# Two output projections of a hybrid decoder by one level of Strassen's algorithm, with weight sums made in DRAM

## The chip, the core and the metric

The kernel runs on one core of a Trainium2 chip. The metric is device microseconds (us) of one execution; lower is better. The core has TensorE (PE, with its weight loads PEld), VectorE (DVE), ScalarE (ACT), GpSimd (POOL) and SyncE (SP, which issues the DMAs of the kernel before). "Granted clock" is TensorE's clock as the records show it, as a share of 2.4 GHz.

## The reference

Two decoder layers over 1024 tokens of width 1024, in float32. Layer 0 is a gated DeltaNet, layer 1 a Mamba-2 SSD mixer. Each ends in an output projection of 2048 channels to 1024, which is what is changed here, then a residual sum and the next norm.

```python
def reference(x, norm_w, ...):                       # x: 1 x 1024 x 1024
    hid = rmsnorm(x, norm_w[0])
    o = gated_deltanet_core(hid, gdn_w_in, ...)      # 1024 x 2048, 16 heads of 128
    x = x + o @ gdn_w_out                            # gdn_w_out: 2048 x 1024
    hid = rmsnorm(x, norm_w[1])
    y = ssd_core(hid, ssd_w_in, ...)                 # 1024 x 2048, 8 groups of 256
    x = x + y @ ssd_w_out                            # ssd_w_out: 2048 x 1024
    return rmsnorm(x, final_norm_w)
```

## The kernel before

Every large matmul is made of three: an operand is split into a rounded part (hi, float32r, a cast on ACT) and the rest (lo, a subtraction on DVE; `split`, lines 86 and 87), and hi x hi, hi x lo and lo x hi are summed in PSUM. Tokens come in 8 chunks n of 128.

The stages are: norm of x into `hid` (hi and lo, transposed, in the pool `apool`, tags a0 to a3); the DeltaNet stage in the pool `gw` (8 head pairs g; for each a scan over the 8 chunks, with the inverse and the input projections of later pairs set between its steps, "SIJ"); the first output projection; the SSD stage in the pool `sw` (8 groups g, each a scan over the chunks); the second output projection. In the scan of the last pair or group there are no input projections left; only the z matmuls (lines 227 to 229) of its 8 chunks stand between the steps of chunks 0 to 3. A scan ends for each chunk in `store`: transposes, a copy into `yg`, and a DMA to y0d (line 691) or y1d (line 923). In the DeltaNet scan the recurrence runs over lines 626 (S times k), 629, 634, 637, 643 and 649 (new S); its output over 661 to 680.

`out_proj` (line 321) takes each half of 512 outputs in turn (nh), in it the 8 chunks n, in them 4 blocks kq of 512 channels: it loads a block of y (line 340) and splits it, and makes 12 matmuls of 128 x 512 (lines 347 to 349). The weights of the first half lie in apool and those of the second in `bpool`, which is opened when gw is closed and stays open through the SSD stage. With nh = 0 the sums go to DRAM (`keep`: x1d or xfd); with nh = 1 a row of 1024 is complete, is normed (`rms_first`, `rms_second`) and goes to `on_rows`: transposes into `hid2` through `to_hid` in the middle, the output at the end. Rows, norms and the norm weights nw lie in `nrm1` and `nrm2`.

Pools lie on a stack: one that is opened after another has been closed takes the same bytes. Instructions are ordered on each engine by a planner that simulates the program; an engine then runs its own list strictly in order. Tiles of one tag share a fixed number of buffers (`bufs`).

## Time and profile before

| | |
|---|---|
| Median of 3 runs | 1993.75 us (1992.37 to 1995.21) |
| The profiled execution | 1990.66 us, span of the core 1989.0 us |
| Mean granted clock | 0.987 |
| Busy share of the span | PE 96%, PEld 82%, DVE 66%, ACT 53%, POOL 21% |
| DMA | 34.2% of 16 engines, all of it on one queue (SP's) |

The span runs from the first to the last instruction of the core in one profiled execution. A matmul's end is modelled and matmuls are pipelined, so that their listed durations overlap. An idle engine costs nothing unless another waits for it.

### The profile page before, as it was taken

What the parts mean: (1) busy time and instruction counts of PE and PEld (TensorE: products, weight loads), DVE (VectorE), ACT (ScalarE), POOL (GpSimd) and SP (SyncE); (2) the same over time, 40 slices, a digit from 0 to 9 for tenths busy, and PEclk for the clock granted to TensorE, in tenths of its full rate; (3) what the DMA queues carried; (4) which work ended last, traced back from release to release, by engine and by line L of the source; (5) the groups of instructions that cost most, each with busy time, mean ns of one, the idle gap of its engine ahead of it and who ended that gap; (6) DMA issues with size and microseconds to landing.
All of it is one profiled execution on the core that took longest, in us unless ns stands there. A gap on an engine that the chain in (4) does not pass through costs nothing.

```text
span 1989.0 us, 36043 instructions
## 1 busy us (share of the span) xinstructions
PE 1919.1 (96%) x12974; PEld 1639.7 (82%) x12974; DVE 1305.7 (66%) x2915; ACT 1063.4 (53%) x2893; POOL 411.6 (21%) x818
## 2 busy tenths in 40 slices
PE   7997999999999999999999999999999999999998
PEld 5786888888888888897778788888888888888886
DVE  6797685778677776844354676657666676767333
ACT  5635656575656666564343554544555555555332
POOL 1101211212122212100000032423333243332000
PEclk9997999999999999999999999999999999999999
DMA  4421323232232323235574232222222223236654
GB/s 141 117 54 49 98 56 84 67 78 75 57 93 52 99 49 105 58 94 157 152 221 133 64 91 80 69 84 80 64 80 57 80 75 83 78 104 195 203 170 142
DMA packets 284789, 193.35 MB, mean 97 GB/s; under 512 B 65425, under 2 KB 246338, under 8 KB 284610
## 3 DMA queue, kind: packets, MB, share of 16 engines
q1 hardware_dynamic: 284610, 191.05, 34.2%
q8 instruction: 102, 1.67, 0.4%
q14 instruction: 77, 0.63, 0.1%
HBM read 159.34 MB, written 31.65 MB: 96 GB/s over the span
## 4 chain that ended last, share of the span: by engine, by line
PE 75%; DMA 9%; DVE 7%; ACT 4%; POOL 2%; issue 2%; SPq 1%; POOLq 0%; DVEq 0%; ACTq 0%
PE ps_proj L165 9%; PE ps_proj L166 9%; PE ps_proj L167 9%; PE ps_proj L347 6%; PE ps_proj L349 6%; PE ps_proj L348 5%; PE ps_proj L227 5%; PE ps_proj L228 4%; PE ps_proj L229 4%; DMA gcrow<-gcr_s 2%; PE ps_tr L66 2%; PE ps_pt L66 2%; DMA X<-xd 2%; DVE acc L204 2%; PE ps_sc L895 1%
## 5 line engine op out<-in xcount | busy, mean ns | idle before, releaser
L165 PE MATMUL ps_proj<-hid_h,wh 128*128 128x512 f32 x1024 | 412.9, 403 | 3.4 <-ACT acc L200 3.2
L167 PE MATMUL ps_proj<-hid_h,wl 128*128 128x512 f32 x1024 | 404.9, 395 | 0.0
L166 PE MATMUL ps_proj<-hid_l,wh 128*128 128x512 f32 x1024 | 403.6, 394 | 0.0
L227 PE MATMUL ps_proj<-zh,hid_h 128*128 128x256 f32 x1024 | 300.5, 293 | 1.0 <-DVE z L234 1.0
L229 PE MATMUL ps_proj<-zh,hid_l 128*128 128x256 f32 x1024 | 295.4, 288 | 0.0
L228 PE MATMUL ps_proj<-zl,hid_h 128*128 128x256 f32 x1024 | 295.4, 288 | 0.0
L165 PEld LDWEIGHTS ps_proj<-hid_h,wh 128*128 128x128 f32 x1024 | 192.7, 188 | 43.9 <-ACT acc L200 4.0
L167 PEld LDWEIGHTS ps_proj<-hid_h,wl 128*128 128x128 f32 x1024 | 192.5, 188 | 40.3
L166 PEld LDWEIGHTS ps_proj<-hid_l,wh 128*128 128x128 f32 x1024 | 192.9, 188 | 35.4
L347 PE MATMUL ps_proj<-woh,yh 128*128 128x512 f32 x512 | 205.2, 402 | 4.6 <-ACT yh L86 3.2
L348 PE MATMUL ps_proj<-wol,yh 128*128 128x512 f32 x512 | 204.4, 400 | 0.8 <-DVE wol L87 0.7
L349 PE MATMUL ps_proj<-woh,yl 128*128 128x512 f32 x512 | 203.1, 399 | 0.8 <-DVE yl L87 0.7
L227 PEld LDWEIGHTS ps_proj<-zh,hid_h 128*128 128x128 f32 x1024 | 196.3, 192 | 6.0 <-DVE z L234 2.3
L228 PEld LDWEIGHTS ps_proj<-zl,hid_h 128*128 128x128 f32 x1024 | 196.4, 192 | 3.0
L229 PEld LDWEIGHTS ps_proj<-zh,hid_l 128*128 128x128 f32 x1024 | 196.4, 192 | 0.3
L204 DVE SCALAR_TENSOR_TENSOR acc<-raw,cw_ssd,acc 128x512 f32<-128x512 f32 x192 | 156.5, 815 | 45.2 <-ACT acc L202 42.5
L86 ACT CAST yh<-yr 128x512 fp32r<-128x512 f32 x128 | 79.1, 619 | 142.2 <-PE ps_proj L348 90.8
L87 DVE TENSOR_TENSOR yl<-yr,yh 128x512 fp32r<-128x512 f32 x128 | 89.0, 696 | 98.7 <-ACT yh L86 98.3
L204 DVE SCALAR_TENSOR_TENSOR acc<-raw,cw_gdn,acc 128x512 f32<-128x512 f32 x192 | 145.9, 761 | 11.8 <-ACT acc L200 10.2
L87 DVE TENSOR_TENSOR wl<-wr,wh 128x512 fp32r<-128x512 f32 x128 | 89.3, 698 | 68.3 <-ACT wh L86 67.7
L317 POOL TENSOR_SCALAR_AFFINE_SELECT gcrow<-gcrow 128x512 f32<-128x512 f32 x128 | 92.1, 722 | 197.1 <-DMA gcrow<-gcr_g 141.8
L676 POOL TENSOR_SCALAR so<-so,cq 128x2 f32<-128x2 f32 x64 | 27.3, 426 | 462.7 <-ACT yn L675 462.7
(240 smaller groups left out, 3872.0 us busy)
## 6 DMA issues: line engine op xcount, KB each, us to landing
wr<-in_gdn_w_in_dram SPq DMA_DIRECT2D x96, 256.0 KB, 3.0
wr<-in_ssd_w_in_dram SPq DMA_DIRECT2D x96, 256.0 KB, 2.9
gcrow<-gcr_g SPq DMA_DIRECT2D x64, 256.0 KB, 3.6
yr<-y0d SPq DMA_DIRECT2D x64, 256.0 KB, 3.4
gcrow<-gcr_s SPq DMA_DIRECT2D x64, 256.0 KB, 3.9
yr<-y1d SPq DMA_DIRECT2D x64, 256.0 KB, 3.2
y0d<-yg SPq DMA_DIRECT2D x64, 128.0 KB, 1.9
wr<-in_gdn_w_out_dram SPq DMA_DIRECT2D x32, 256.0 KB, 3.5
```

The source lines that it names most:

```text
L87: nc.vector.tensor_tensor(out=lo, in0=src, in1=hi.bitcast(F32), op=ALU.subtract)
L165: nc.tensor.matmul(pt[0:nco], hi[:, j, 0:nco], xh[:, j, :], start=first, stop=False)
L166: nc.tensor.matmul(pt[0:nco], hi[:, j, 0:nco], xl[:, j, :], start=False, stop=False)
L167: nc.tensor.matmul(pt[0:nco], lo[:, j, 0:nco], xh[:, j, :], start=False, stop=last)
L204: nc.vector.scalar_tensor_tensor(out=acc, in0=raw[:, k:k + 512], scalar=cw[:, k * 32 + ti:k * 32 + ti + 1], in1=acc, op0=ALU.mult, op1=ALU ...
L227: nc.tensor.matmul(pt, xh, zh[:, k, :], start=k == 0, stop=False)
L228: nc.tensor.matmul(pt, xh, zl[:, k, :], start=False, stop=False)
L229: nc.tensor.matmul(pt, xl, zh[:, k, :], start=False, stop=k == KT - 1)
L317: nc.gpsimd.affine_select(out=t, in_=t, pattern=[[0, 4], [1, P]], compare_op=ALU.is_ge, fill=-1e30, base=0, channel_multiplier=-1)
L347: nc.tensor.matmul(pt, yh[:, j, :], hi[:, j, :], start=first, stop=False)
L348: nc.tensor.matmul(pt, yh[:, j, :], lo[:, j, :], start=False, stop=False)
L349: nc.tensor.matmul(pt, yl[:, j, :], hi[:, j, :], start=False, stop=last)
```

## The change

Tokens, channels and outputs are each cut in two. Instead of 8 products of halves there are 7, each of 512 tokens x 1024 channels x 512 outputs (8 pieces j of 128 channels, 4 banks p of 128 tokens), of sums of quarters of y and sums of quarters of the weights. The sums of y are made on the way: in a tile T and on POOL and DVE (`y_form`). Four sums of weight quarters for each projection (s1 to s4) are made in DRAM while the DeltaNet stage runs: `weight_sums` yields 11 DMAs from POOL's queue for each projection, 4 that copy 2 MB and 7 that add 2 MB to what is there; one is traced at every second slot of the scans. Weights are split again for each product instead of once.

The products alternate between two sets of four PSUM banks (U and V). Sums of products are kept in rows of 1024 that start from the residual (8 tiles of 512 KB, loaded when product 0 is done), and in u. Products 5 and 6 complete four rows each. All tiles of the new `out_proj` but the raw loads are in nrm1 and nrm2; bpool is opened for the SSD stage alone, and closed with it. y is stored in four quarters of 1024 channels x 512 tokens, so that its rows are 2 KB instead of 512 bytes.

The diff, without lines that are only removed from `out_proj`:

```diff
--- before.py
+++ after.py
...
-    def rms_first(pool, xrow):
-        xn = pool.tile([P, D], F32, tag="xn", name="xn")
-        ss = st.tile([P, 2], F32, tag="ss2", name="ss2")
-        nc.scalar.activation(xn[:, 0:512], xrow[:, 0:512], AF.Square, accum_out=ss[:, 0:1])
+    def rms_first(sq, xrow, c):
+        ss = st.tile([P, 2], F32, tag="ss2", name="ss2", bufs=NT)
+        nc.scalar.activation(sq, xrow[:, c * 512:(c + 1) * 512], AF.Square, accum_out=ss[:, 0:1])
         nc.gpsimd.tensor_scalar(out=ss[:, 0:1], in0=ss[:, 0:1], scalar1=1.0 / D, scalar2=EPS, op0=ALU.mult,
                                 op1=ALU.add)
-        return xn, ss
-
-    def rms_second(xrow, xn, ss, nw, emit):
-        nc.scalar.activation(xn[:, 512:1024], xrow[:, 512:1024], AF.Square, accum_out=ss[:, 1:2])
+        return ss
+
+    def rms_second(xrow, xn, ss, nw, emit, c):
+        cs = slice(c * 512, c * 512 + 512)
+        nc.scalar.activation(xn[:, cs], xrow[:, cs], AF.Square, accum_out=ss[:, 1:2])
...
     def to_hid(kh, xn, hid, n):
-        pt = (ps_pt, ps_sc)[kh]()
+        pt = (ps_tr, ps_sc)[kh]()
...
-    def out_proj(yd, w_out, resid, wpools, npool, nw, on_rows, keep):
...
+    def weight_sums(w_out, nm):
+        X = lambda c, k: w_out[k * 1024:(k + 1) * 1024, c * 512:(c + 1) * 512]
+        parts = {"s1": ((1, 0), (1, 1)), "s2": ((1, 0), (1, 1), (0, 0)), "s3": ((0, 0), (1, 0)),
+                 "s4": ((0, 1), (1, 0), (1, 1), (0, 0))}
+        forms = {f"x{c}{k}": X(c, k) for c in range(2) for k in range(2)}
+        for f in parts:
+            forms[f] = tc.dram_tile([1024, 512], F32, name=f"wo_{nm}{f}")
+        def steps():
+            for i in range(4):
+                for f, p in parts.items():
+                    if i < len(p):
+                        if i == 0:
+                            nc.gpsimd.dma_start(forms[f], X(*p[0]))
+                        else:
+                            nc.gpsimd.dma_start(forms[f], X(*p[i]), accum_op=ALU.add)
+                        yield
+        return forms, steps()
+    def out_proj(yd, forms, resid, npool, nw, on_rows):
+        rows = {t: [npool.tile([P, D], F32, tag="xr", name="xrow", bufs=NT) for _ in range(4)] for t in range(2)}
+        tok = lambda t, p: p + 4 * (1 - t)
+        Tt = npool.tile([P, 8, 512], F32, tag="T", name="Tt", bufs=1)
+        sums = {}
+        def load_y(k, t, j):
+            yr = cv.tile([P, 512], F32, tag="acc", name="yr", bufs=3)
+            nc.sync.dma_start(yr, yd[k, 1 - t][j * P:(j + 1) * P, :])
+            return yr
+        def y_form(i, j):
+            if i == 0:
+                return load_y(0, 0, j)
+            if i == 3:
+                return load_y(1, 0, j)
+            if i == 5:
+                return load_y(1, 1, j)
+            if i == 4:
+                a, b = load_y(1, 1, j), load_y(0, 1, j)
+                nc.gpsimd.tensor_tensor(out=a, in0=a, in1=b, op=ALU.subtract)
+                return a
+            d = Tt[:, j, :]
+            if i == 1:
+                a, b = load_y(0, 0, j), load_y(0, 1, j)
+                nc.gpsimd.tensor_tensor(out=d, in0=a, in1=b, op=ALU.subtract)
+            elif i == 2:
+                a = load_y(1, 1, j)
+                nc.vector.scalar_tensor_tensor(out=d, in0=d, scalar=-1.0, in1=a, op0=ALU.mult, op1=ALU.subtract)
+            else:
+                a = load_y(1, 0, j)
+                nc.vector.scalar_tensor_tensor(out=d, in0=d, scalar=-1.0, in1=a, op0=ALU.mult, op1=ALU.subtract)
+            return d
+        def pieces(i, j):
+            raw = wring.tile([P, 512], F32, tag="wr", name="wr", bufs=3)
+            nc.sync.dma_start(raw, forms[wf[i]][j * P:(j + 1) * P, :])
+            wh = npool.tile([P, 512], F32R, tag="woh", name="woh", bufs=4)
+            wl = npool.tile([P, 512], F32R, tag="wol", name="wol", bufs=4)
+            split(wh, wl, raw)
+            y = y_form(i, j)
+            yh = npool.tile([P, 512], F32R, tag="yh", name="yh", bufs=4)
+            yl = npool.tile([P, 512], F32R, tag="yl", name="yl", bufs=4)
+            split(yh, yl, y)
+            return wh, wl, yh, yl
+        def mac(pt, pc, p, first, last):
+            wh, wl, yh, yl = pc
+            c = slice(p * P, (p + 1) * P)
+            nc.tensor.matmul(pt, yh[:, c], wh, start=first, stop=False)
+            nc.tensor.matmul(pt, yh[:, c], wl, start=False, stop=False)
+            nc.tensor.matmul(pt, yl[:, c], wh, start=False, stop=last)
+        def product(i, banks, done):
             for j in range(4):
+                pc = pieces(i, j)
+                for p in range(4):
+                    mac(banks[p], pc, p, j == 0, False)
+            pcs = [pieces(i, j) for j in range(4, 8)] if i == 6 else None
+            if i == 6:
+                for p in range(4):
                     for j in range(4):
+                        mac(banks[p], pcs[j], p, False, j == 3)
+                    done(p, banks[p])
+                return
+            for j in range(4, 8):
+                pc = pieces(i, j)
+                for p in range(4):
+                    mac(banks[p], pc, p, False, j == 7)
+            for p in range(4):
+                done(p, banks[p])
+        def put(t, p, c, pt, op):
+            v = rows[t][p][:, c * 512:(c + 1) * 512]
+            if op == ALU.add:
+                nc.vector.tensor_tensor(out=v, in0=pt, in1=v, op=ALU.add)
+            else:
+                nc.vector.tensor_tensor(out=v, in0=v, in1=pt, op=ALU.subtract)
+        def finish(t, p, c):
+            xrow = rows[t][p]
+            on_rows(tok(t, p), xrow, lambda emit: rms_second(xrow, npool.tile([P, D], F32, tag="xn", name="xn"),
+                                                             sums[t, p], nw, emit, c))
+        def first(t, p, c):
+            sums[t, p] = rms_first(npool.tile([P, 512], F32, tag="sq", name="sq", bufs=1), rows[t][p], c)
+        wf = ("x00", "s1", "s2", "x01", "s3", "s4", "x11")
+        U = lambda: [ps_proj(), ps_proj(), ps_pt(), ps_pt()]
+        V = lambda: [ps_tr(), ps_tr(), ps_sc(), ps_sc()]
+        u = npool.tile([P, 4, 512], F32, tag="u", name="u", bufs=1)
+        def put_u(t, p, c, op):
+            v = rows[t][p][:, c * 512:(c + 1) * 512]
+            nc.gpsimd.tensor_tensor(out=v, in0=v, in1=u[:, p, :], op=op)
+        def grow(p, pt):
+            nc.vector.tensor_tensor(out=u[:, p, :], in0=pt, in1=u[:, p, :], op=ALU.add)
+        def d0(p, pt):
+            for t in range(2):
+                nc.sync.dma_start(rows[t][p], resid(tok(t, p)))
+            nc.scalar.copy(u[:, p, :], pt)
+            put(0, p, 0, pt, ALU.add)
+        def d1(p, pt):
+            put(1, p, 0, pt, ALU.add)
+            put(1, p, 1, pt, ALU.subtract)
+        def d2(p, pt):
+            grow(p, pt)
+            put_u(1, p, 0, ALU.add)
+        def d3(p, pt):
+            put(0, p, 0, pt, ALU.add)
+            first(0, p, 0)
+        def d4(p, pt):
+            grow(p, pt)
+            put_u(1, p, 1, ALU.subtract)
+            first(1, p, 1)
+            put_u(0, p, 1, ALU.subtract)
+        def d5(p, pt):
+            put(1, p, 0, pt, ALU.add)
+            finish(1, p, 0)
+        def d6(p, pt):
+            put(0, p, 1, pt, ALU.subtract)
+            finish(0, p, 1)
+        for i, done in enumerate((d0, d1, d2, d3, d4, d5, d6)):
+            product(i, V() if i % 2 else U(), done)
...
-    yd0 = [tc.dram_tile([2048, P], F32, name=f"y0d{n}") for n in range(NT)]
+    def y_dram(nm):
+        return {(k, t): tc.dram_tile([1024, 512], F32, name=f"{nm}{k}{t}") for k in range(2) for t in range(2)}
+
+    def y_cut(yd, g, n):
+        return yd[g // 4, n // 4][(g % 4) * 256:(g % 4 + 1) * 256, (n % 4) * P:(n % 4 + 1) * P]
+
+    yd0, yd1 = y_dram("y0d"), y_dram("y1d")
+    wo0, steps0 = weight_sums(gw_out, "g")
+    wo1, steps1 = weight_sums(sw_out, "s")
...
-                nc.sync.dma_start(yd0[n][g * 256:(g + 1) * 256, :].rearrange("(h p) t -> p h t", p=P), yg)
+                nc.sync.dma_start(y_cut(yd0, g, n).rearrange("(h p) t -> p h t", p=P), yg)
...
             for slot in range(8):
+                if slot % 2:
+                    next(steps0 if g < 3 else steps1, None)
                 for c in "SIJ":
...
-    bpool = ctx.enter_context(tc.tile_pool(name="bpool", bufs=2))
     hid2 = hid_tiles(apool)
 
     with tc.tile_pool(name="nrm1", bufs=2) as nrm:
         nw = load_nw(nrm, norm_w[1])
 
         def rows_mid(n, xrow, norm):
-            nc.sync.dma_start(x1d[n][:, 512:1024], xrow[:, 512:1024])
+            nc.sync.dma_start(x1d[n], xrow)
             norm(lambda kh, xn: to_hid(kh, xn, hid2, n))
 
-        out_proj(yd0, gw_out, lambda n: x[n * P:(n + 1) * P, :], (apool, bpool), nrm, nw, rows_mid, x1d)
-
-    yd1 = [tc.dram_tile([2048, P], F32, name=f"y1d{n}") for n in range(NT)]
-    xfd = [tc.dram_tile([P, D], F32, name=f"xfd{n}") for n in range(NT)]
-
-    with tc.tile_pool(name="sw", bufs=2) as sw:
+        out_proj(yd0, wo0, lambda n: x[n * P:(n + 1) * P, :], nrm, nw, rows_mid)
+
+    with tc.tile_pool(name="bpool", bufs=2) as bpool, tc.tile_pool(name="sw", bufs=2) as sw:
...
-        out_proj(yd1, sw_out, lambda n: x1d[n], (apool, bpool), nrm, nw, rows_last, xfd)
+        out_proj(yd1, wo1, lambda n: x1d[n], nrm, nw, rows_last)
```

## Rows read from the trace of the kernel before

**Rows 1.** the page, part 1: engine, busy us (share of the span) x instructions.
```profile
PE 1919.1 (96%) x12974; PEld 1639.7 (82%) x12974; DVE 1305.7 (66%) x2915; ACT 1063.4 (53%) x2893; POOL 411.6 (21%) x818
```

**Rows 2.** windows: stretch, length, busy us of PE, PEld, DVE, ACT, POOL; clock, DMA, GB/s.
```profile
160.00:200.00 40.00, 31.28 (x162) 25.81 (x163) 34.47 (x105) 23.05 (x87) 5.95 (x13) 0.78 0.10 32
...
985.00:1030.00 45.00, 42.15 (x171) 31.62 (x171) 23.86 (x38) 21.39 (x41) 2.02 (x6) 0.96 0.86 248
...
1844.00:1960.00 116.00, 116.00 (x504) 94.42 (x503) 45.54 (x69) 36.97 (x72) 5.40 (x17) 1.00 0.62 184
```

**Rows 3.** instructions of lines L349 and L229 (the latter from 840 to 900 us).
```profile
L349 PE MATMUL ps_proj<-woh,yl x512: 387/395/629, 886.0 to 1981.5; 128*128 128x512 f32 x171
...
L229 PE MATMUL ps_proj<-zh,hid_l x66: 273/282/387, 839.7 to 885.5; 128*128 128x256 f32 x66
```

**Rows 4.** windows of line L347 alone: busy us (x instructions) of PE and PEld, clock, DMA.
```profile
889.00:985.20 96.20, 44.11 (x107) 20.52 (x107) 0.98 0.49 148
...
1797.00:1843.30 46.30, 21.45 (x55) 10.16 (x54) 1.00 0.71 213
```

**Rows 5.** timeline of PE, 163 to 190 us: start us, us, what, idle before.
```profile
173.50 1.22 PE L634 MATMUL ps_sc<-vpp,nte 128*128 128x128 f32 x4 [0.80 <-DVE vpp L629]
...
179.29 0.71 PE L634 MATMUL ps_sc<-vpp,nte 128*128 128x128 f32 x4 [0.70 <-DVE vpp L629]
```

**Rows 6.** chain that ended last, 880 to 1120 us: start us, us, what.
```profile
891.78 0.44 PE ps_sc L634 x4
...
933.49 0.45 PE ps_sc L634 x4
...
1107.77 0.44 PE ps_sc L66 x4
```

**Rows 7.** timeline of all engines, 963 to 968 us.
```profile
963.76 0.42 DVE L671 TENSOR_TENSOR o<-ps_sc,o 128x256 f32<-128x256 f32 x1 [0.67 <-ACT o L670]
...
965.65 0.61 PE L634 MATMUL ps_sc<-vpp,nte 128*128 128x128 f32 x4
...
966.48 0.62 DVE L680 SCALAR_TENSOR_TENSOR yn<-o,so,z 128x128 f32<-128x128 f32 x2 [2.29 <-POOL so L678]
```

**Rows 8.** chain that ended last, 955 to 1000 us.
```profile
981.22 3.95 DMA y0d<-yg
...
985.27 0.63 ACT woh L86
```

**Rows 9.** instructions on tile nw: count, ns min/median/max, first to last start.
```profile
L91 SPq DMA_DIRECT2D nw<-in_norm_w_dram x2: 345/382/420, 1.2 to 985.2; - x2
...
L91 SPq DMA_DIRECT2D nw<-in_final_norm_w_dram x1: 333/333/333, 1844.0 to 1844.0; - x1
```

**Rows 10.** groups by line: xcount, busy us, mean ns of one, idle before.
```profile
L87 DVE TENSOR_TENSOR yl<-yr,yh 128x512 fp32r<-128x512 f32 x128 | 89.0, 696 | 98.7 <-ACT yh L86 98.3
...
L887 POOL TENSOR_TENSOR S<-S,egl_s 128x256 f32<-128x256 f32 x48 | 37.8, 788 | 24.0 <-DVE S L888 17.1 <-DVE S L885 2.8 <-PE ps_tr L66 2.5
```

**Rows 11.** timeline of all engines, 1790 to 1846 us.
```profile
1793.92 0.27 PE L895 MATMUL ps_sc<-xs,mt 128*64 128x64 f32 x1
...
1827.77 0.27 PE L895 MATMUL ps_sc<-xs,mt 128*64 128x64 f32 x1
...
1832.84 0.35 DVE L910 TENSOR_SCALAR yn<-y,so 128x256 f32<-128x256 f32 x1
```

**Rows 12.** DMA issues: count, KB each, median us to landing.
```profile
yr<-y1d SPq DMA_DIRECT2D x64, 256.0 KB, 3.2
...
xrow<-in_x_dram SPq DMA_DIRECT2D x8, 512.0 KB, 7.9
```

**Rows 13.** timeline of POOL, first 8 us.
```profile
1.49 0.10 POOL L194 MEMSET raw<- 128x3 f32 x1
...
6.07 0.19 POOL L99 TENSOR_SCALAR rr<-ss 128x1 f32<-128x1 f32 x1 [4.25 <-ACT xn L97]
```

More of the change, by code (lines that the diff above doesn't have):

```diff
@@ L319, in gc_rows @@
         return t
-    def out_proj(yd, w_out, resid, wpools, npool, nw, on_rows, keep):
-        def load_kq(nh, kq):
-            hi = wpools[nh].tile([P, 4, 512], F32R, tag=("a0", "a0", "a1", "a1")[kq], name="woh", bufs=2)
-            lo = wpools[nh].tile([P, 4, 512], F32R, tag=("a2", "a2", "a3", "a3")[kq], name="wol", bufs=2)
-            for j in range(4):
-                k = kq * 4 + j
-                raw = wring.tile([P, 512], F32, tag="wr", name="wr", bufs=3)
-                nc.sync.dma_start(raw, w_out[k * P:(k + 1) * P, nh * 512:(nh + 1) * 512])
-                split(hi[:, j, :], lo[:, j, :], raw)
-            return hi, lo
-        w = {(0, kq): load_kq(0, kq) for kq in range(4)}
-        for nh in range(2):
-            for n in range(NT):
-                if nh == 0 and n >= 4:
-                    w[1, n - 4] = load_kq(1, n - 4)
-                pt = ps_proj()
-                for kq in range(4):
-                    yr = cv.tile([P, 4, P], F32, tag="acc", name="yr", bufs=3)
-                    nc.sync.dma_start(yr, yd[n][kq * 512:(kq + 1) * 512, :].rearrange("(k p) t -> p k t", p=P))
-                    yh = wring.tile([P, 4, P], F32R, tag="wh", name="yh")
-                    yl = wring.tile([P, 4, P], F32R, tag="wl", name="yl")
-                    split(yh, yl, yr)
-                    hi, lo = w[nh, kq]
-                    for j in range(4):
-                        first, last = kq == 0 and j == 0, kq == 3 and j == 3
-                        nc.tensor.matmul(pt, yh[:, j, :], hi[:, j, :], start=first, stop=False)
-                        nc.tensor.matmul(pt, yh[:, j, :], lo[:, j, :], start=False, stop=False)
-                        nc.tensor.matmul(pt, yl[:, j, :], hi[:, j, :], start=False, stop=last)
-                xin = cv.tile([P, 512], F32, tag="th", name="xin")
-                nc.sync.dma_start(xin, resid(n)[:, nh * 512:(nh + 1) * 512])
-                if nh == 0:
-                    nc.vector.tensor_tensor(out=xin, in0=pt, in1=xin, op=ALU.add)
-                    nc.sync.dma_start(keep[n][:, 0:512], xin)
-                else:
-                    xrow = npool.tile([P, D], F32, tag="xr", name="xrow")
-                    nc.sync.dma_start(xrow[:, 0:512], keep[n][:, 0:512])
-                    xn, ss = rms_first(npool, xrow)
-                    nc.vector.tensor_tensor(out=xrow[:, 512:1024], in0=pt, in1=xin, op=ALU.add)
-                    on_rows(n, xrow, lambda emit: rms_second(xrow, xn, ss, nw, emit))
@@ L922, in store @@
                                          scale=snw[:, 2 * g + i:2 * g + i + 1])
-                nc.sync.dma_start(yd1[n][g * 256:(g + 1) * 256, :].rearrange("(h p) t -> p h t", p=P), yg)
+                nc.sync.dma_start(y_cut(yd1, g, n).rearrange("(h p) t -> p h t", p=P), yg)
             S = None
```

## Prediction

> **What bounds the kernel now.** I read the page's busy table first: PE is busy 1919 of 1989 us, POOL a fifth of that [rows 1]. PE's figure overstates its work, since matmuls overlap, so the second view is the windows: in a stretch that holds nothing but the second output projection, 504 matmuls took 116.0 us, 0.230 us each [rows 2], although one of them is listed with 0.395 [rows 3]. At that pace PE has no free time there. Each of the projections' three lines has 512 matmuls [rows 3], so a projection has 768, 177 us of pure matmul time.
>
> Third, where that work lies. L349 starts first at 886.0 us, just behind the last matmul for z (L229, 885.5), and last at 1981.5 [rows 3]. So the first projection starts while head pair 7 of the DeltaNet scan is still going, and the second while group 7 of the SSD scan is. L347 alone has 107 matmuls between 889 and 985.2, and 55 between 1797 and 1843.3 [rows 4]; with its two partners that is 321 and 165, 74 and 38 us of PE work, laid between the steps of a scan that by itself leaves PE waiting. What such a scan looks like with hardly any filler stands at 160 to 200 us: PE busy 31 of 40 us, DVE 34, the mean granted clock 0.78, so part of it at 1.2 instead of 2.4 GHz [rows 2]; there two steps of the recurrence (L634) start 5.8 us apart [rows 5]. With the projection between them, two of the last steps took 32 us (933.49 to 965.65) [rows 6, 7].
>
> Fourth, why the projection can start there. Its first-half weights lie in apool, over the hid tiles. The second-half weights lie in bpool, on the bytes of the closed pool gw, and the chain shows their first cast at 985.27, directly behind the last store of the scan, 981.22 + 3.95 us [rows 8]. The loads of nw for nrm1 and nrm2, which lie on bytes of the same kind, issue at 985.2 and 1844.0, each as its scan's last store lands [rows 9]. So here every tile of a new pool waited for the last user of the pool whose bytes it took.
>
> **The change part by part.** *Matmuls.* Seven products of 8 x 4 x 3 are 672 for 768: 96 fewer per projection, 22.1 us, 44.2 for both. Same shapes and the same order of weight loads, so the same 0.230.
>
> *The cover that goes.* woh, wol, yh and yl now come from nrm1 and nrm2, and T, u, the rows and xn too. By [rows 8, 9] nothing of product 0 can be split before the scan's last store has landed. The first two products need only channels of groups 0 to 3, which were written long before, but that frees nothing. In the first projection chain step 2 stands at 891.78 [rows 6]; I put it at 890 without matmuls ahead of it. Five unfilled steps of 5.9 end at 919.5. From step 7 to the store: L634 to its output about 2.5 us, the output tile to yn 3.3 (963.76 to the end of the L680 pair, 966.48 + 0.62) [rows 7], transposes and the copy about 0.7, the store 3.95 [rows 8], semaphores: 11 us. Before, from 965.65, it was 19.5 us with filler; that is the upper bound. So the pool opens at 930.5, and after two casts of 0.63 [rows 8] PE starts at 932. Then 2 us for a clock that has fallen, 672 x 0.230 = 155, and 7 us of transposes (16 groups of 0.44): 1096. Before, the last transposes end at 1108.2 [rows 6], since the second-half weights also cost a stall there (985 to 1030: 171 matmuls and transposes in 45 us, DMA share 0.86 [rows 2]). Gain of the first: 12 us, not 22.
>
> In the second, main step 3 is at 1793.92 and step 7 at 1827.77 [rows 11], filled steps 8.5 us apart. POOL has three products of 0.79 in a step, 2.4 us, as the floor [rows 10]. I take 4.85, a little under the middle, as most of a filled step is filler: step 7 at 1813.3. Step 7 to the last yn was 5.4 us before (1827.77 to 1832.84 + 0.35) [rows 11], transposes and copies 1.2, the store 4: 1823.9. PE starts at 1825.4, and 1.5 us of slow clock and 155 us end at 1982, where the old one ended. Gain: none. Together 12 us.
>
> *Feeding the products.* A product lasts 22.1 us, a piece (12 matmuls) 2.76. A piece takes two casts of 0.63 on ACT and two subtractions of 0.70 on DVE [rows 8, 10], well inside. Products 2 and 3 add eight combinations on T at the same 0.70: DVE 16.8 us, and the puts of the product before up to 5.6 more. Product 6 of the first projection is worse: after product 5 four rows are finished at once, 4 x (0.7 + 1.4 + 1.4) = 14 us of DVE ahead of its own 11.2, more than 22.1. Products 1 and 4 need two y loads in three buffers, each held for a landing of 3.2 us [rows 12], a POOL subtraction (about 1.5 us, twice the 0.79 of half the size [rows 10]) and a split: about 4 us a piece where PE wants 2.76, of which the four pieces of lead hide only part. Product 0 starts while eight rows of 512 KB are fetched too; such eight took 7.9 us each at the start [rows 12]. Below, all of it hides in the lead but 3 us for both projections. Above: product 1 late by 11, 4 by 4, 6 by 4 and the start by 4, 23 in the first and 12 in the second. I take 10 and 6, nearer the middle, since the start empties the lead.
>
> *Weight sums.* 22 transfers of 2 MB leave from POOL's queue, 14 of them accumulating. No row shows a DMA from POOL. Its list is not in program order: the memset of the first convolution (L194) stands at 1.49, before the norm's L99 at 6.07, and a transfer without a predecessor may be placed as early as that [rows 13]. Below, they cost nothing: POOL is idle 79% [rows 1]. Above: 2 MB at 248 GB/s [rows 2] is 8.5 us, and if POOL or a scan's small loads are held for that long, a quarter of 22 times reaches PE: 47 us. I take 6, near the lower end, as only the stretches with a wait for POOL or a load feel it.
>
> The Trainium skill, "SBUF — State Buffer", section "SBUF: two separate sides", has a rule against this change: a DMA issued from GpSimd has its descriptors written by GpSimd, and a VectorE instruction that holds the shared port keeps it from writing them. No run here shows it. The page's example (620 ns alone, 3100 beside a copy) would give, as an estimate from that page, 22 x 2.5 = 55 us on POOL's queue, and a time up to 2053 if all of that came through.
>
> *The rest.* The stores and reloads of keep and xfd that go cost PE nothing now. bpool opens after nrm1; its first user gtmp waited for the end of the same matmuls before. What follows the last matmul keeps its parts.
>
> **Sum.** -12 + 16 + 6 = +10 us. The profiled execution took 1990.66, of which 1989.0 is span; the runs' median is 1993.75, 0.15% higher, and the same work stands in both, so I add to the median: 2004.
>
> **Rivals.** *The lead hides the feeding* (faster). Stalls of 3 us for both, weight sums free: -9; if the scan's tail is 3 us shorter in each than I make it: -15, so 1979 to 1985. For: PE had no gap in 1844 to 1960 with 184 GB/s moving [rows 2]. Against: products 1 and 4 want half as much again. It decides from the point where feeding and weight sums together cost under 8 us. *The scan keeps its cover* (faster still): if a tile waited only for its own bytes, product 0 would fill some 21 us of each scan: 10 - 42, 1962. [rows 8, 9] speak against it. *POOL's queue becomes a bound* (much slower): an accumulating transfer must wait for the one before it on the same sum, and that wait stands ahead of gcrow masks, conv edges and norms in POOL's queue, for which ACT and DVE wait: 47 instead of 6, 2045. For: POOL's list may take them early; against: other sums lie between two steps of one. *All cancels*: within 0.2%.
>
> **How the numbers follow.** 0.2% (4 us) is about what a measurement of this kernel can tell from no change. Forecast (lost cover, some feeding stalls) 0.46, POOL's queue 0.14: slower 0.60. Cancelled 0.15. Hidden feeding 0.20 and kept cover 0.05: faster 0.25. The forecast's own range is 1998 to 2025. To leave out no more than 2 in 10, the range reaches into the hidden feeding and up to the upper price of the weight sums: 1978 to 2045.
>
> **What will show it.** Right: the first cast of woh directly behind the last y store; PE nearly idle for 30 us ahead of it, with a fallen clock; about 165 us from the first to the last matmul of a projection; gaps in products 1, 4 and 6. Wrong: product matmuls before the last store; projections of 156 us with no gap; a DeltaNet stage stretched by more than 10 us.

## The result and the profile after

The changed kernel took 2173.24 us (median of four runs, 2168.95 to 2182.44), the kernel before 1993.06 us beside it: a ratio of 1.0909, interval [1.0871, 1.0947], or 180 us more. The forecast was 2004, its range ended at 2045. The profiled execution took 2182.44 us with a span of 2180.7, where before had 1989.0: 191.7 more.

The page of the changed kernel, its busy table, the slices that matter and its DMA queues:

```profile
PE 1914.4 (88%) x12782; PEld 1621.3 (74%) x12782; DVE 1385.1 (64%) x3011; ACT 1083.8 (50%) x2933; POOL 524.0 (24%) x896
...
PE   2722789999999999999779999999999999997897
...
PEclk6766789999999999999999999999999999997999
DMA  9999531323232222222366623232222213215665
...
q1 hardware_dynamic: 237762, 201.54, 31.8%
q0 software_dynamic: 18784, 46.14, 9.8%
```

PE has 192 instructions fewer than in [rows 1], as forecast, and is busy 88% instead of 96%. The loss stands in the first four slices (218 us): PE at 2 to 7 tenths, the DMA engines at 9. Two later dips, in slices 20 and 21 and in 37 and 38, are the starts of the two projections. q0 is the queue of POOL's transfers: 9.8% of 2180.7 us is 214 us of all sixteen DMA engines.

The windows of the start, first of the changed kernel, then of the kernel before (columns as in [rows 2]: length; busy us and count of PE, PEld, DVE, ACT, POOL; clock, DMA share, GB/s):

```profile
0.00:20.00 20.00, 3.31 (x16) 3.07 (x16) 4.55 (x5) 7.81 (x13) 10.53 (x26) 0.94 0.92 345
40.00:60.00 20.00, 2.47 (x6) 1.25 (x7) 0.69 (x4) 0.40 (x1) 2.58 (x2) 0.50 1.03 321
120.00:140.00 20.00, 0.00 (x0) 0.00 (x0) 0.00 (x0) 0.00 (x0) 1.39 (x1) 0.50 1.12 228
180.00:200.00 20.00, 0.00 (x0) 0.00 (x0) 0.75 (x1) 0.00 (x0) 1.51 (x3) 0.54 1.13 207
```

```profile
0.00:20.00 20.00, 7.82 (x32) 6.28 (x32) 9.98 (x13) 11.05 (x20) 4.89 (x21) 1.00 0.76 259
40.00:60.00 20.00, 20.00 (x102) 16.35 (x102) 14.70 (x45) 10.32 (x18) 0.23 (x2) 1.00 0.20 54
120.00:140.00 20.00, 19.51 (x101) 16.50 (x100) 18.50 (x43) 8.26 (x16) 0.57 (x4) 1.00 0.27 54
```

From 120 to 140 us no compute engine does anything but POOL, which issues one transfer, and the granted clock stands at 0.50, the 1.2 GHz level, behind stretches in which PE had little to do. The same 20 us of before are nearly full. The transfers themselves, grouped by line and tile (durations in ns are POOL's time to issue one; below them the landing times, minimum, median and maximum, first of the copies, then of the accumulating ones):

```profile
L335 POOL DMA_DIRECT2D wo_gs<-in_gdn_w_out_dram x4: 777/784/1042, 1.8 to 4.3; - x4
L335 POOL DMA_DIRECT2D wo_ss<-in_ssd_w_out_dram x4: 774/774/774, 5.1 to 7.3; - x4
...
DMA to landing us min/median/max: 16.1/42.8/69.4
```

```profile
L337 POOL DMA_DIRECT2D wo_gs<-in_gdn_w_out_dram x7: 1272/1337/1413, 18.2 to 196.3; - x7
...
DMA to landing us min/median/max: 25.2/76.9/93.4
```

All eight copies have left by 8 us, as early as [rows 13] allowed. The last accumulating one leaves at 216.5. What the loads of SP find meanwhile, from the DMA issues of 0 to 220 us (count, size, median us to landing), before and after:

```profile
wr<-in_gdn_w_in_dram SPq DMA_DIRECT2D x25, 256.0 KB, 2.9
```

```profile
q0 software_dynamic: 17762, 44.08, 91.5%
q1 hardware_dynamic: 9698, 9.07, 14.6%
...
wr<-in_gdn_w_in_dram SPq DMA_DIRECT2D x11, 256.0 KB, 19.0
gcrow<-gcr_g SPq DMA_DIRECT2D x4, 256.0 KB, 21.1
```

A weight load of 256 KB lands in 19.0 us instead of 2.9, and 11 of them are issued in the time of 25. The last y0d store is issued at 1072.3 us (981.2 before, with the projection's filler among the steps), the first projection's last matmul ends at 1261.2 (before 1099.5, +161.7), the second's at 2169.1 (1981.9, +187.2), the span at 2180.7 (+191.7). By the matmuls of L165, which both kernels have, 152 us are lost by 269 us; most of the rest goes in the second projection. So the DeltaNet stage was stretched by far more than the 10 us that the prediction named as a sign of being wrong.

### The profile page after: what moved, and what is told of

The parts are those of the page before. It is cut to its first block, busy times and chain, and to the rows that moved or that the text cites. A ratio compares the mean times of both kernels' runs of the same rounds, so it can differ in the third digit from the quotient of the medians.

```text
span 2180.7 us, 36007 instructions
## 1 busy us (share of the span) xinstructions
PE 1914.4 (88%) x12782; PEld 1621.3 (74%) x12782; DVE 1385.1 (64%) x3011; ACT 1083.8 (50%) x2933; POOL 524.0 (24%) x896
## 5 line engine op out<-in xcount | busy, mean ns | idle before, releaser
L165 PE MATMUL ps_proj<-hid_h,wh 128*128 128x512 f32 x1024 | 415.5, 406 | 50.9 <-ACT wh L86 45.9
L229 PE MATMUL ps_proj<-zh,hid_l 128*128 128x256 f32 x1024 | 297.8, 291 | 0.0
L165 PEld LDWEIGHTS ps_proj<-hid_h,wh 128*128 128x128 f32 x1024 | 194.8, 190 | 93.3 <-ACT wh L86 47.0
L229 PEld LDWEIGHTS ps_proj<-zh,hid_l 128*128 128x128 f32 x1024 | 197.6, 193 | 0.5
L184 ACT ACTIVATE th<-acc 128x512 f32<-128x512 f32 x128 | 80.1, 627 | 119.8 <-DVE acc L204 119.4
L197 ACT COPY raw<-ps_proj 128x512 f32<-128x512 f32 x128 | 74.3, 580 | 99.6 <-PE ps_proj L167 95.1
L86 ACT CAST wh<-wr 128x512 fp32r<-128x512 f32 x128 | 78.3, 615 | 88.9 <-PE ps_proj L166 56.5
L609 DVE TENSOR_TENSOR tm<-Dt,X 128x2 f32<-128x2 f32 (+30 forms) x248 | 86.9, 350 | 45.3 <-POOL X L598 40.0
L87 DVE TENSOR_TENSOR wol<-wr,woh 128x512 fp32r<-128x512 f32 x112 | 86.3, 774 | 44.7 <-ACT woh L86 44.4
```

The costliest lines, as they stand in the source:

```text
L86: nc.scalar.copy(hi, src)
L87: nc.vector.tensor_tensor(out=lo, in0=src, in1=hi.bitcast(F32), op=ALU.subtract)
L165: nc.tensor.matmul(pt[0:nco], hi[:, j, 0:nco], xh[:, j, :], start=first, stop=False)
L184: nc.scalar.activation(th, src, AF.Tanh, scale=0.5)
L229: nc.tensor.matmul(pt, xl, zh[:, k, :], start=False, stop=k == KT - 1)
L609: nc.vector.tensor_tensor(out=tv, in0=Dt[:, r0:, s:], in1=X[:, s:s + 1, s:].to_broadcast([P, nr, nj]), op=ALU.mult)
```

## The experiments

Every kernel is compared with the kernel before on its own chip (1992.5 to 1999.8 us there). "Over before" is the difference of the medians; the ratio is estimated from all the runs of both kernels and need not be exactly that of the medians. Besides the changed kernel itself, only e1, e11 and e14 use the whole sums; e2 makes them, and nothing reads them. The others leave some or all of the sums out, so that some of their products are of other weights; they are there for their times.

| run | us | over before | ratio, interval |
|---|---|---|---|
| changed kernel | 2173.24 | +180.2 | 1.0909 [1.0871, 1.0947] |
| e2, sums alone in the kernel before | 2143.12 | +143.3 | one run |
| e3, no sums | 2034.40 | +34.6 | 1.0179 [1.0162, 1.0196] |
| e4, copies, nothing accumulates | 2152.86 | +153.1 | one run |
| e5, eight copies | 2061.66 | +66.2 | one run |
| e10, eight big copies | 2144.10 | +145.2 | one run |
| e1, sums spread over the DeltaNet stage | 2092.24 | +92.4 | 1.0464 [1.0443, 1.0485] |
| e11, small sums over both scans, nine y buffers | 2042.76 | +43.9 | 1.0211 [1.0190, 1.0233] |
| e6, no sums, nine y buffers | 2001.08 | +5.7 | 1.0035 [1.0024, 1.0047] |
| e7, no sums, product 0 as cover | 2032.75 | +37.3 | 1.0189 [1.0170, 1.0208] |
| e9, e6 and e7 | 2010.80 | +11.9 | 1.0052 [1.0031, 1.0072] |
| e8, e6, rows by program order | 2003.46 | +8.0 | 1.0043 [1.0029, 1.0058] |
| e12, e6, rows behind y loads | 2000.04 | +7.5 | 1.0043 [1.0028, 1.0057] |
| e13, e6, rows behind weight loads | 2016.93 | +17.9 | 1.0085 [1.0070, 1.0100] |
| e14, e11 and e13 | 2043.91 | +44.9 | 1.0237 [1.0203, 1.0271] |

### What the weight sums cost, and why

**e1.**

```diff
-                            nc.gpsimd.dma_start(forms[f], X(*p[0]))
+                            d = nc.gpsimd.dma_start(forms[f], X(*p[0]))
...
+                        tc.keep_in_program_order(d)
                         yield
```

> The changed kernel with one difference: each of the 22 weight-sum transfers is kept behind the instruction that stands ahead of it in the program on POOL's queue, so that they leave one by one between the scan's slots instead of eight at once at 1.8 us. Theory H (the transfers, all at the start, fill the DMA engines for 240 us, and the loads of the first stage wait behind them): the 157 us that the DeltaNet stage lost come back, less what single transfers of 2 MB cost in the scans: 2016 to 2040 us. Rival Q (POOL's in-order queue, which waits at each accumulating transfer for the one before it, is what holds the others): the waits now stand inside the scans, 14 of some 5 to 9 us: 2050 to 2120 us. Rival R (it is the new order of the other instructions that costs, not the transfers): about 2173 us.

**e2.** The kernel before, with `weight_sums` and the calls of `next(steps0 ...)` in its slots.

> The kernel before with nothing but the 22 weight-sum transfers added, at the same places in the program; nothing reads the sums. H and Q both: they leave at the start again, 1993 + 157 = about 2150 us, nearly all of it lost before 250 us. R: within 15 us of the kernel before, 1990 to 2010 us.

**e3.**

```diff
-            forms[f] = tc.dram_tile([1024, 512], F32, name=f"wo_{nm}{f}")
+            forms[f] = X(*parts[f][0])
...
-                        if i == 0:
-                            nc.gpsimd.dma_start(forms[f], X(*p[0]))
-                        else:
-                            nc.gpsimd.dma_start(forms[f], X(*p[i]), accum_op=ALU.add)
                         yield
```

> The changed kernel without any weight-sum transfer: products 1, 2, 4 and 5 read plain quarters of the weights in place of the sums (so these four products are of other weights). H and Q: the DeltaNet stage runs as before, and what is left is what the two projections themselves cost: 2173 - 157 = 2016 us; by the terms of the prediction it would be 2004 - 6 = 1998 us. R: about 2170 us.

**e4.**

```diff
-                            nc.gpsimd.dma_start(forms[f], X(*p[i]), accum_op=ALU.add)
+                            nc.gpsimd.dma_start(tc.dram_tile([1024, 512], F32, name=f"wo_{nm}{f}{i}"), X(*p[i]))
```

> The changed kernel with every accumulating transfer replaced by a plain copy of the same 2 MB quarter into a DRAM tile of its own: 22 copies, the same places in the program, no transfer that has to wait for another (products 1, 2, 4, 5 so read first copies instead of sums). H: 22 copies still move 46 MB each way at the start, so most of the loss stays, 2100 to 2170 us, and POOL has no waits. Q: without the waits the stage runs nearly as before, 2016 to 2050 us.

e2 and e3 agree: the sums cost 143.3 us in the kernel before and 180.2 - 34.6 = 145.6 in the changed one. R falls; it is the transfers. e1 came out above H's 2040 and inside Q's range of 2050 to 2120: with the sums spread, they still cost 92.4 - 34.6 = 57.8. But POOL waits for none of the transfers in e1, so these 57.8 us are not Q's waits. e4 did not tell H from Q as it was meant to. POOL waited for transfers there too, 97 us in all, although no copy needs another (why, the runs do not show), and PE's longest pause ended behind POOL's part of the first norm (engine and line, for what: us, times, longest; 0 to 180 us):

```profile
PE ps_tr L66 <- DVE xn L101: 96.7, 5, 89.5
DVE xn L101 <- POOL rr L100: 88.0, 2, 87.8
```

Hence two kernels whose transfers make POOL wait for nothing.

**e5** is the changed kernel without the `else` branch, so without any accumulating transfer.

> The changed kernel with only the eight first transfers of the sums, plain 2 MB copies that all leave by 8 us and for which POOL waits at nothing (products 1, 2, 4 and 5 read these copies instead of sums). Theory H (bytes ahead of the first loads): a copy alone lands in 10.5 us, so eight hold the DMA engines for some 84 us; the 118 us that 22 copies cost over no sums, times 8/22, is 43: about 2077 us, lost before 100 us. Rival Q (POOL's waits hold the stage): no waits, so as without sums, 2034 to 2040 us.

e5, a single run, lost 66.2 - 34.6 = 31.6 us: below H's 43, but far above Q's 6 at most.

**e10** is e3 with eight copies of columns of the input weights.

```diff
+        big = [tc.dram_tile([1024, 1408], F32, name=f"big_{nm}{c}") for c in range(4)]
         def steps():
+            for c in range(4):
+                nc.gpsimd.dma_start(big[c], w_big[:, c * 1408:(c + 1) * 1408])
+                yield
+            return
```

> The changed kernel without weight sums, as e3, and in their place eight plain copies of 5.8 MB (columns of the input weights into DRAM tiles that nothing reads), 46.1 MB as the 22 transfers write, all leaving POOL by 8 us, none waiting for another. Theory H (bytes ahead of the first loads): about what 22 copies of 2 MB cost over no sums, 118 us: 2110 to 2155 us. Rival Q (POOL's waits between the transfers hold the stage): POOL waits for nothing, so no more than the eight small copies: 2034 to 2065 us.

e10, a single run too, shows what the bytes do alone. The same groups for its transfers, its window of 40 to 60 us, and two of its waits from 0 to 220 us:

```profile
L334 POOL DMA_DIRECT2D big_g<-in_gdn_w_in_dram x4: 751/766/1030, 1.8 to 4.3; - x4
L334 POOL DMA_DIRECT2D big_s<-in_ssd_w_in_dram x4: 751/751/751, 5.1 to 7.3; - x4
its engine sat idle before it (us, times) until:
who waited for it (us, times):
...
DMA to landing us min/median/max: 30.0/98.4/165.7
```

```profile
40.00:60.00 20.00, 0.00 (x0) 0.00 (x0) 1.01 (x5) 0.23 (x1) 0.06 (x1) 0.50 0.96 322
```

```profile
PE ps_proj L262 <- DVE wg L87: 33.0, 1, 33.0
ACT wg L86 <- DMA wraw<-in_gdn_w_in_dram: 25.3, 1, 25.3
```

Nothing stands under "sat idle": POOL waits for none of them and has issued all by 8 us. Yet 145.2 - 34.6 = 110.6 us are lost, PE does nothing from 40 to 60 us, and the DMA share is 0.96. PE's longest pause, 33.0 us, ends behind the landing of a load (wraw). So H's mechanism is enough for a loss of 110.6 us: bytes in front of the first loads.

In the changed kernel Q's mechanism is there as well (timeline of POOL, in brackets the idle time ahead and its releaser): a copy and a memset for the convolutions come 48 us behind the instruction before them.

```profile
105.41 0.25 POOL L585 TENSOR_SCALAR skh<-skh 128x8 f32<-128x8 f32 x1
129.33 1.39 POOL L337 DMA_DIRECT2D wo_gs<-in_gdn_w_out_dram  x1 [23.67 <-DMA wo_gs<-in_gdn_w_out_dram]
152.89 1.29 POOL L337 DMA_DIRECT2D wo_ss<-in_ssd_w_out_dram  x1 [22.17 <-DMA wo_ss<-in_ssd_w_out_dram]
153.65 0.72 POOL L196 COPY raw<-raw 128x3 f32<-128x3 f32 x1
153.77 0.65 POOL L194 MEMSET raw<- 128x3 f32 x1
```

The two waits of 24 and 22 us end with the landing of a transfer. These waits reach PE (the changed kernel's waits from 0 to 240 us):

```profile
DVE acc L204 <- POOL raw L194: 74.4, 3, 40.8
ACT lt L542 <- POOL gcrow L317: 50.1, 2, 49.9
PE ps_proj L165 <- ACT wh L86: 45.9, 3, 41.5
PE ps_pt L66 <- DVE nte L575: 45.2, 1, 45.2
```

PE's two longest pauses, 41.5 and 45.2 us, end here, at 159.1 and 223.4 us. Ahead of the first stand the memset at 153.77 on POOL, sums on DVE and then instructions of ACT; the three weight loads issued before it, at 101.4 to 102.6 us, had taken at most 24.4 us to land. Ahead of the second stand the masks of gcrow on POOL at 217.3, behind the last transfer, though gcrow's loads had been issued by 114.7 us and took at most 22.3. So both pauses, 86.7 us, end behind POOL's queue and not behind a load. What was lost before them went with late loads (wraw landed in 27.8 us, before in 3.8). The DMA engines were full over the whole 220 us besides, and e10 shows what that costs alone. What each mechanism would cost in the changed kernel without the other, and with it the 145.6 - 110.6 = 35 us that are left, was not separated; accumulating transfers on a queue on which nothing else waits were not tried.

The share of the software queue times the span gives the time of the transfers' packets on all DMA engines. Against it, the cost over the same kernel without sums is (e5, e10 and e4 are single runs):

| run | DMA time, us | cost, us | share that reaches the end |
|---|---|---|---|
| e5 | 2.4% x 2060.0 = 49 | 31.6 | 0.64 |
| e10 | 6.2% x 2142.4 = 133 | 110.6 | 0.83 |
| e4 | 6.6% x 2151.2 = 142 | 118.5 | 0.83 |
| changed kernel | 9.8% x 2180.7 = 214 | 145.6 | 0.68 |
| e1, spread | 10.7% x 2092.9 = 224 | 57.8 | 0.26 |
| e11, small, both scans (over e6) | 11.8% x 2042.0 = 241 | 38.2 | 0.16 |

At the start some two thirds to five sixths of the transfers' time reach the end, whichever way they hold PE; in the scans it is a quarter to a sixth.

**e11.**

```diff
+                    for r in range(4 if i < len(p) else 0):
+                        s = slice(r * 256, r * 256 + 256)
...
+                            d = nc.gpsimd.dma_start(forms[f][s, :], X(*p[i])[s, :], accum_op=ALU.add)
+                        tc.keep_in_program_order(d)
...
             for slot in range(8):
+                next(steps1, None)
                 next(S, None)
```

> The whole change, with e6's nine y buffers, and with the weight sums in 88 transfers of 512 KB, kept in program order on POOL's queue: one per slot, those of the first projection in the DeltaNet scan, those of the second in the SSD scan. Theory H (the price is what small loads wait behind a long transfer): a small load waits at most 4 us instead of 10 to 16, and the SSD scan has few loads on its path: e6's 2001 plus 10 to 25 us, 2011 to 2026 us. Rival (the price goes by the bytes, wherever they are): e1's 58 us on e6: about 2059 us. Rival (it goes by the number of transfers on POOL): more than 2080 us.

The 38 us over e6 are above the expected 10 to 25 and below the 58 of the rival. The DeltaNet scan ends 33 us later than in e6 (last y0d store at 959.5 instead of 926.6), and by the matmuls of L165 the SSD scan loses another 9, with the same 44 transfers each. In the DeltaNet scan the waits (engine and line, for what: us, times, longest) show whom they hold:

```profile
DVE tm L614 <- POOL X L603: 40.8, 6, 9.7
POOL X L603 <- DMA X<-xd: 37.9, 6, 13.8
ACT lt L547 <- POOL gcrow L317: 34.4, 10, 10.0
```

In e6 these are 26.7, 21.4 and 12.8 us. X and gcrow are round trips through DRAM on the path of the inverses, and cutting the transfers in four did not shelter them. POOL's own time to issue the 44 transfers of a stage (medians 0.56 us for a copy, 1.00 to 1.03 for an accumulating one, some 37 us in all) stands ahead of its work too; it was not separated from the DMA engines' time.

### What the projections cost without the sums

e3's 34.6 us belong to the projections. Times from the first matmul of a product to the first of the next (the last to its last matmul), first and second projection:

```
             product 0     1     2     3     4     5     6    first  last matmul
e3  first      28.4  31.5  22.2  21.8  26.6  23.4  30.9    925.1  1109.8
    second     28.6  33.2  22.4  21.8  26.5  23.4  26.2   1836.3  2018.4
e6  first      28.1  23.1  21.8  21.8  21.8  26.0  25.5    929.7  1097.7
    second     29.5  22.3  21.8  21.8  21.8  27.1  21.9   1822.0  1988.1
e9  first      69.5  26.7  28.3  21.8  21.8  26.6  25.5    884.2  1104.3
    second     55.6  26.9  28.9  21.8  21.8  28.3  21.9   1794.4  1999.6
e13 first      26.0  25.1  28.2  21.8  21.8  28.3  25.5    934.0  1110.6
    second     25.4  24.2  26.9  21.8  21.8  27.1  21.9   1836.0  2005.1
```

Product 1 of e3, second projection, in the chain that ended last (start, us, what):

```profile
1871.75 1.29 POOL Tt L365
1873.06 3.38 DMA yr<-y1d
1876.51 1.27 POOL Tt L365
1877.79 2.63 DMA yr<-y1d
1880.56 1.29 POOL Tt L365
1881.87 2.57 DMA yr<-y1d
```

A load of 2.6 to 3.4 us and a subtraction of 1.3 take turns, 4.0 to 4.8 us a piece.

**e6.**

```diff
-            yr = cv.tile([P, 512], F32, tag="acc", name="yr", bufs=3)
+            yp, yt = ((cv, "acc"), (wring, "wh"), (wring, "wl"))[ny[0] % 3]
+            ny[0] += 1
+            yr = yp.tile([P, 512], F32, tag=yt, name="yr", bufs=3)
```

> The changed kernel without weight sums, as e3, with the y tiles of the products taken in turn from three rings of three buffers instead of one. Theory B (three buffers let only one pair of y loads go at a time, so that a piece of products 1 and 4 takes a load of 2.7 and a subtraction of 1.3 us in turn, 4.0 instead of 2.76): products 1 and 4 fall from 31 to 33 and 26.5 us to 23 to 24, 2034 - 24 = about 2010 us. Rival D (the DMA engines or the subtraction itself are the limit): within 8 us of e3, 2026 to 2036 us.

B holds: products 1 and 4 fall to 21.8 to 23.1, and the ratio from 1.0179 to 1.0035. Products 2 to 4 now run with no gap. Product 5 has become longer (26.0, 27.1): PE waits there for DVE, which is busy 24.3 of 26 us with combinations on T, `grow` and splits.

**e7** takes the tiles of product 0 from apool, with hid2 allocated at its first use.

```diff
+            if i == 0:
+                if j % 4 == 0:
+                    ap.update({k: apool.tile([P, 4, 512], F32R, tag=t, name=n, bufs=2) for k, t, n in
+                               (("wh", "a0", "woh"), ("wl", "a2", "wol"), ("yh", "a1", "yh"), ("yl", "a3", "yl"))})
```

> The changed kernel without weight sums, as e3, with the split tiles of product 0 in the old pool apool instead of the new pools nrm1 and nrm2, so that no wait for the closed pool stands ahead of them. Theory C (the wait for the closed pool costs the cover): matmuls of product 0 start some 30 us ahead of the last y store, fill part of both scan tails, and 22 us of matmuls per projection move there less the lengthening of the steps: 2034 - 25 = 2000 to 2020 us. Rival: the steps of the scans grow by as much as is filled in (before, filled steps took 7.6 to 8.5 us, unfilled 5 to 5.9): 2030 to 2038 us.

e7 came to 2032.75, inside its rival's range: nothing was gained over e3.

**e9** is both edits.

> The changed kernel without weight sums, with e6's nine y buffers and e7's tiles of product 0 in apool together. Theory C and B: in e7 what product 0 won was lost again in product 1, 42 us long, since its loads stood behind the new pool with three y buffers; with nine buffers that falls by some 10 us: 8 to 15 us below e6, 1986 to 1993 us. Rival (the scan steps pay for what is filled in, and the rest waits for the new pool anyway): within 5 us of e6, 1996 to 2006 us.

In e9 the theory falls as well: 8 to 15 us below e6 were expected, and it came 6 above (11.9 against 5.7 over before; the two intervals overlap). Its 2010.80 is even above its rival's 1996 to 2006. What the rivals said of the scan is in the trace. Matmuls of product 0 now start 45 us ahead in the DeltaNet tail, but the tail grows by as much. Its windows, e9 to its last store and e6 to its own:

```profile
884.00:947.00 63.00, 53.15 (x314) 45.23 (x312) 25.38 (x72) 28.93 (x103) 7.86 (x16) 0.98 0.21 70
```

```profile
884.00:927.00 43.00, 30.80 (x207) 25.78 (x205) 18.24 (x59) 22.23 (x87) 7.70 (x16) 0.96 0.07 22
```

The 107 PE instructions more, 22 us of work, made the stretch 20 us longer. What is saved is some 2 us, and products 1 and 2, with their loads behind the new pool, give back more: the first projection ends at 1104.3 instead of 1097.7.

**e8, e12, e13** try to move the eight row loads out of product 0, in which e6's DMA share is 1.02. e8 keeps them in program order, e12 behind the eighth y load, e13 behind the eighth weight load:

```diff
-            for t in range(2):
-                nc.sync.dma_start(rows[t][p], resid(tok(t, p)))
+            with tc.issue_after(w0[7].ins):
+                for t in range(2):
+                    nc.sync.dma_start(rows[t][p], resid(tok(t, p)))
```

> As e6, with the eight loads of 512 KB for the rows kept behind the loads of product 0 on SP's queue, as they stand in the program. Theory B with the start as a term of its own: product 0 falls from 28.5 us to 23 to 24 in both projections, 8 to 10 us below e6. Rival: product 0 is slow because it starts with empty buffers and a fallen clock, not because of the rows: within 4 us of e6.

> As e6 (no weight sums, nine y buffers), with the eight row loads of 512 KB issued behind the eighth y load of product 0 on SP's queue; e8's edit had left them where they were. Theory (the rows crowd the first loads: the DMA engines are full for the 28 us of product 0): product 0 falls from 28.1 and 29.5 us to 23 or 24 in both projections, 8 to 10 us below e6, so a ratio to the kernel before of about 0.999. Rival (product 0 is slow because its first pieces start from nothing, with a fallen clock, and the rows are then late for the sums behind it): within 4 us of e6, a ratio of 1.002 to 1.006.

> As e6 (no weight sums, nine y buffers), with the eight row loads of 512 KB issued behind the eighth weight load of product 0, so that they no longer stand ahead of its weights on SP's queue. Theory (the rows crowd the first loads): product 0 falls from 28.1 and 29.5 us to 23 to 25 in both projections, 6 to 11 us below e6: a ratio to the kernel before of 0.998 to 1.0005. Rival (the rows are only late somewhere else, for the sums behind product 0): the gain comes back as a gap in product 1 or 2, a ratio of 1.002 to 1.006.

In e8 and e12 the rows still leave at the opening of the pool (927.9 to 936.9 in e12), since what they were put behind had left long before; the two say nothing about the question. In e13 they leave from 943.5 on. Product 0 becomes 2 to 4 us shorter, but product 1 becomes 2 longer and product 2 some 5 to 6, and the whole is slower. So the gap came back in products 1 and 2, as the rival said, and more than came back: 1.0085 is above the rival's 1.006 too. That these bytes have to come within the first products wherever they stand fits, but was not shown.

**e14** is e11 with this edit.

> The whole change as in e11 (nine y buffers, weight sums in 88 transfers of 512 KB over both scans), with e13's place of the row loads. By the theory e11's ratio 1.0211 less 0.004: 1.017, still above the kernel before, since the sums alone cost 40 us there. Rival (the sums' price was that of crowded first loads as well): 1.010 or less.

1.0237, above what either side expected and not better than e11. No version, with the sums or without, was faster than the kernel before.

## Why the prediction was wrong, step by step

**The step that failed** is the price of the weight sums: "a quarter of 22 times reaches PE: 47 us. I take 6, near the lower end". It measured 146. The size of one transfer was nearly right (22 x 8.5 = 187 against 214 us of DMA time). What was wrong is the share, and it goes by the place. Where the transfers are spread over the scans (e1), 0.26 of their time reaches the end, 57.8 us: about the quarter that was the upper bound. At the start it is 0.68. The text had the early place of the transfers [rows 13] and yet took a scan's share as its upper bound and POOL's idle time over the whole span [rows 1] as its lower one. The 6 was taken because "only the stretches with a wait for POOL or a load feel it"; at the start of the changed kernel that is most of the time (PE is busy 81 of the first 220 us). Only the first 20 us of the kernel before are bound by loads (DMA share 0.76, PE at 7.8 of 20); from 40 to 60 us PE is full at a DMA share of 0.20. It is the 46 MB put in front that hold the loads behind them, and POOL's waits for these transfers that hold what stands behind them on its list.

**POOL's queue as a bound**, the rival at 2045, had the right place and sign, and its mechanism is in the trace: conv edges and gcrow masks stand behind the waits, and 86.7 us of PE's pauses end there. What spoke against it, that "other sums lie between two steps of one", did not help: POOL waited 151 us for transfers in twelve waits. But it is not the only cause, as e10 loses 110.6 us without any such wait, and its 47 us was too little for either.

The Trainium skill, "DMA: Bandwidth & Descriptors", section "Issuing engines are not separate DMA queues", says that transfers of any issuer end up on the same 16 engines and interleave. The trace agrees: SP's weight loads land in 19.0 us instead of 2.9 beside POOL's transfers. The rule of the Trainium skill that the prediction cited, from "SBUF — State Buffer", section "SBUF: two separate sides", shows nothing of the estimate's size in POOL's issue times. In e1, where the transfers leave amid the scans, POOL needs 0.76 to 1.04 us for a copy and 1.34 to 1.43 for an accumulating one, about 26 us for all 22, where the estimate had 55 us of waiting alone; at the start of the changed kernel, with VectorE mostly idle, it needs 0.77 to 1.04 and 1.27 to 1.41. Whether VectorE held the port in e1, no run shows.

**Feeding** was mis-sized as well: taken 10 + 6. From the first to the last matmul, where about 165 us were to show, e3 has 184.7 and 182.1 us. With 155 of matmuls, 2 and 1.5 of slow clock and 7 of transposes in the first, 20.7 and 25.6 are stalls, where the upper ends were 23 and 12. The 4 us a piece were right, and so were the places: products 0, 1, 4 and 6. What failed is the middle that was taken, and the 12 for the second projection, half of the first without a reason. The text counted on "which the four pieces of lead hide only part"; in product 1 the lead hid nothing of it (9.7 and 11.4 us over 21.8, upper end 11), in product 4 about half (4.8 and 4.7). That product 1 has no lead because product 0 is late fits, but was not tested. Nine buffers return 29 us (1.44% of 1996).

**The cover that goes** was right in mechanism, and within 7 us in size. The first cast of woh stands right behind the landing of the last y store, as in [rows 8], and PE waits for it (timeline of the changed kernel):

```profile
1072.34 0.36 SPq L815 DMA_DIRECT2D y0d<-yg  x1
1074.24 0.62 ACT L86 CAST woh<-wr 128x512 fp32r<-128x512 f32 x1 [1.93 <-DMA y0d<-yg]
...
1075.48 1.19 PE L393 MATMUL ps_proj<-woh,yh 128*128 128x512 f32 x2 [4.79 <-ACT yh L86]
```

The first projection was to start at 932; in e3 it does at 925.1 and in e6 at 929.7. The second was to start at 1825.4, and in e6 it does at 1822.0. With the stalls of products 1 and 4 gone (e6), the first projection ends at 1097.7, forecast 1096. PE was not nearly idle ahead of it, though: 20.61 of 32 us from 1040 to 1072, at a clock of 0.95. The clock did fall in the second tail, to 0.77 from 1960 to 1985.

**The scan keeps its cover**, the rival at 1962, was refused for the right reason and priced wrongly: its 42 us took the fill as free, and e9 shows that the scan pays for it.

**The matmuls**: 21.8 us a product in steady flow, forecast 22.1. Right.

**What follows the last matmul** "keeps its parts": it took 11.6 us (2169.1 to 2180.7) instead of 7.1, 4.5 us more than foreseen. Product 6 finishes four rows in a row, and in the chain at the end a norm (ACT xn) waits for the landing of an earlier row's output; no run separates this.

Without the sums, these steps come to 1994 + 35 = 2029 by e3, inside the range; the sums alone carry it to 2173.

## What to carry to other kernels

A transfer with nothing ahead of it was placed at the very start here, so price it there: against the time that it fills the DMA engines while other loads are wanted, and against everything that stands behind it on the issuing engine's list, not against that engine's idle time. A product saved on the bounding engine is worth only what the feeding can follow: count loads per piece against buffers, with no lead. And filling a latency-bound recurrence with matmuls stretched it here (e9); count the fill as saved only by as much as the stretch stays behind.

## What the runs showed of the hardware

Copies of 2 MB between two places in DRAM landed 10.5 us after their issue when spread (e1, median), accumulating ones in 16.3: by the queue's share an estimate from e5 and the changed kernel is 49 / 8 = 6.2 us of all sixteen DMA engines for one, and (214 - 8 x 6.2) / 14 = 11.7 for the other, nearly twice. Wider rows hardly helped: e10's 46 MB in 5.6 KB rows took 133 us, e4's in 2 KB rows 142, each in one run. And with the transfers cut to a quarter, half of them in the SSD stage (e11), their DMA time was no shorter: 241 us, where e1 had 224.
